# Half-width matmuls in an output projection, a strided operand in another, and some low parts on GpSimd, in a hybrid SSD and convolution decoder layer

## The chip, the cores and the metric

The kernel runs on one core of one Trainium2 chip. The metric is the device time of one execution in microseconds (us). Lower is better. Smaller durations are given in nanoseconds (ns).

## The reference, cut to what matters

One decoder layer is applied to 256 prompt tokens and 8 × 8 sample tokens, which the kernel treats as one set of 320 columns.

```python
x = x + 0.5 * rmsnorm(swiglu_ffn(rmsnorm(x, n_f1_pre), f1g, f1u, f1d), n_f1_post)
m = token_mixer(rmsnorm(x, n_mix_pre), ...)          # and new states
x = x + rmsnorm(m, n_mix_post)
x = x + 0.5 * rmsnorm(swiglu_ffn(rmsnorm(x, n_f2_pre), f2g, f2u, f2d), n_f2_post)

# the end of token_mixer
ssd_out = y @ w_ssd_out                               # y: the SSD scan's output, gated and normed
u = silu(layernorm(u, cc_ln_g, cc_ln_b))              # u: the convolution branch, 1024 channels
cc_out = u @ w_cc_out                                 # (320, 1024) @ (1024, 2048)
g_ssd, g_cc = split(sigmoid(gate_logits), 2)
out = (g_ssd * ssd_out + g_cc * cc_out) @ w_o         # (320, 2048) @ (2048, 2048)
```

The model width is 2048, the width of the feed-forward layers is 5632, and everything is float32.

## The kernel before, in words

**Layout.** Activations lie transposed: 128 channels on the partitions and the `T = 320` tokens along the free dimension. A matmul therefore has a 128 × 128 tile of weights as its stationary operand and 320 columns of activations as its moving operand, and writes 128 × 320 sums to one PSUM bank.

**Precision.** The product of two float32 matrices is made from float32r parts, which the tensor engine streams in one pass. Each operand is split into a high part (a copy rounded to float32r) and a low part (the difference). Three matmuls then make one product: high weights times high activations, low weights times high activations, high weights times low activations. In the code these are `hs` with `xh`, `ls` with `xh`, and `hs` with `xl`.

**Weights.** They are streamed once. SyncE issues a transfer of 512 KB into a buffer `raw` (three of them, each of two chunks of 512 columns). For each chunk ScalarE makes the high part `wh` (six buffers, `split_hi`) and VectorE the low part `wl` (five buffers, `split_lo`), which also ends the use of that half of `raw`. A chunk holds four weight tiles and so feeds 12 matmuls. `ensure` writes these instructions into the program several chunks ahead: when the matmuls of chunk c are written, high parts up to chunk c+6 and low parts up to c+4 have been written (line 210 and 212 issue the transfers).

**Phases.** `phase` runs a matrix product: a list of groups of output tiles (`groups`, mostly two at a time), an inner loop over the `nk` tiles of the contraction, and the three matmuls for each. A function `rhs(k)` names the moving operands and a function `evac` queues the work that empties the PSUM banks, of which there are four (`acc`). The order of phases is: feed-forward 1 in two halves (`w_up1a`, `w_dn1a`, `w_up1b`, `w_dn1b`), the input projections of the mixer, the SSD output projection (`WSSD`), the convolution's output projection (`OUT_16`, 8 tiles of contraction, operands `uh` and `ul` from `rhs_u`, emptied by `evac_cc`, which multiplies by the gate and adds the other branch), the final output projection (`WO`, 16 tiles of contraction, operands `ch` and `cl`, emptied by `evac_o` on ScalarE), and feed-forward 2 (`w_up2a`, `w_dn2a`, `w_up2b`, `w_dn2b`). After the last phase a tail normalizes and adds the result; six of its 16 additions run on GpSimd (line 1454).

**Order.** The order of instructions is written out by the program, with an own model of engine time that decides only where background work (the SSD scan and the convolutions) is placed. All instructions recorded through the wrapped engines carry line 78 in the profile, so tiles rather than lines tell them apart.

Of the kernel before, what the change touches and what calls it, by code (L numbers as in the profile page):

```python
# [6 lines left out]
F32 = mybir.dt.float32  # L7
F32R = mybir.dt.float32r
AF = mybir.ActivationFunctionType
ALU = mybir.AluOpType  # L10

D = 2048
KT = D // 128
T = 320
# [37 lines left out]
WO = [2] * 7 + [1, 1]  # L52


class Bank:
    def __init__(self, ap, now):
        self.ap, self.now = ap, now
        self._free = False
# [111 lines left out]
class Builder:  # L170
    def __init__(self, tc, io):
        self.tc, self.io = tc, io
        self.nc = Core(tc.nc)
        self.clock = self.nc.clock
        self.chunks = []
        for name in (
            "w_up1a", "w_dn1a", "w_up1b", "w_dn1b", "w_in1", "w_dt", "w_in2", "w_ssd", "w_cc", "w_o",
            "w_up2a", "w_dn2a", "w_up2b", "w_dn2b",
        ):
            if name == "w_dt":  # L180
                self.jdt = len(self.chunks)
            for i in range(io[name].shape[0]):
                w = io[name].shape[2]
                for c in range(0, w, CW):
                    self.chunks.append((io[name][i], c, w))
        self.nd = self.nh = self.nl = self.cc = 0
        self.raws, self.spl = {}, {}
        self.tasks, self.bg = [], []
        self.ready = set()
        self.due = []  # L190
        self.slack = 1.4
        self.tick = 0
# [32 lines left out]
    def split_lo(self, j):  # L225
        if j == self.jdt:
            h = self.spl[j][0]
            self.nc.vector.tensor_tensor(h[:, :, 32:64], self.raws.pop(j).rearrange("p (k c) -> p k c", c=32),
                                         h[:, :, 0:32].bitcast(F32), op=ALU.subtract)
            return  # L230
        l = self.wl.tile([128, CW], F32R, name="wl", tag="wl")
        self.nc.vector.tensor_tensor(l, self.raws.pop(j), self.spl[j][0].bitcast(F32), op=ALU.subtract)
        self.spl[j][1] = l

    def prefetch(self, upto):
# [82 lines left out]
        self.cur = self.spl.pop(c)  # L318
        self.cc += 1

    def phase(self, groups, nk, rhs, evac, on_k=None, width=128, on_last=None, mid=None):
        nc = self.nc
        u = 0
        m0 = 0
        per = CW // width
        for gi, G in enumerate(groups):
            if G <= 2:
                accs = [self.ring("acc") for _ in range(G)]
            else:
                accs = [self.ring(t) for t in ("acc", "acc", "acc", "acc", "m", "m", "m")[:G]]  # L330
            for k in range(nk):
                if gi == 0 and on_k is not None:
                    on_k(k)
                for j in range(G):
                    if gi == 0 and j == G - 3 and k == nk - 1 and mid is not None:
                        mid()
                    uu = u % per
                    if uu == 0:
                        self.boundary()
                    if u % 2 == 0:  # L340
                        self.tick += 1
                        self.step_bg()
                    h, l = self.cur
                    hs = h[:, uu * width : (uu + 1) * width]
                    ls = l[:, uu * width : (uu + 1) * width]
                    xh, xl = rhs(k)
                    a = accs[j].ap[:width, :T]
                    nc.tensor.matmul(a, lhsT=hs, rhs=xh, start=(k == 0), stop=False)
                    nc.tensor.matmul(a, lhsT=ls, rhs=xh, start=False, stop=False)
                    nc.tensor.matmul(a, lhsT=hs, rhs=xl, start=False, stop=(k == nk - 1))  # L350
                    u += 1
                if on_last is not None and gi == len(groups) - 1:
                    on_last(k)
            evac(gi, m0, accs)
            m0 += G
# [225 lines left out]
    def mixer(self, on_k):  # L581
        nc, io = self.nc, self.io
# [8 lines left out]
        G1 = lambda m: self.x[:, m]  # L591
# [698 lines left out]
        def rhs_u(k):  # L1290
            assert ("u", k) in self.ready
            uh, ul = st["u"]
            return uh[:, k], ul[:, k]

        ch = [unit("ch0", "A", F32R), unit("ch1", "B", F32R)]
        cl = [unit("cl0", "C", F32R), unit("cl1", "D", F32R)]
# [1 line left out]
        def evac_cc(gi, m0, accs):  # L1298
            def g(m, a):
                t = self.temp()  # L1300
                nc.vector.tensor_tensor(t, a.ap[:, :T], G1(m), op=ALU.mult)
                a.free = True
                nc.vector.tensor_tensor(t, t, G2(m), op=ALU.add)
                yield
                h, l = ch[m // 8][:, m % 8], cl[m // 8][:, m % 8]
                nc.scalar.activation(h, t, AF.Copy)
                yield
                nc.vector.tensor_tensor(l, t, h.bitcast(F32), op=ALU.subtract)
                self.ready.add(("comb", m))
            for i, a in enumerate(accs):  # L1310
                self.tasks.append(g(m0 + i, a))

        self.phase(OUT_16, 8, rhs_u, evac_cc)
        ym = [unit("ym0", "G"), unit("ym1", "H")]
        Y = lambda m: ym[m // 8][:, m % 8]
# [33 lines left out]
                        out=self.x[:, 4 * q : 4 * q + 4], in_=self.xd[:, 4 * q : 4 * q + 4]))  # L1349
            return rhs_c(k)  # L1350

        self.phase(WO, KT, rhs_c2, evac_o)
        self.preload(AF.Sqrt)
        self.flush()
        rb = self.rstd([self.acc_y, self.sq_last], 1.0 / D, keep=True)
# [238 lines left out]
```

## Time and profile before

| | |
|---|---|
| median of the timed runs | 2881.01 us (2 runs, 2880.92 and 2881.09) |
| profiled execution, span from first to last instruction | 2878.3 us |
| profiled execution's time around that span | not recorded; the timed runs' median lies 2.7 us above the span |
| TensorE matmuls | 19597, busy 2857.3 us |
| weight loads | 19597 |
| VectorE, ScalarE, GpSimd busy | 1709.1, 1336.2, 41.1 us |
| stage of `OUT_16` (first to last start) | 1751.7 to 1807.9 us |
| stage of `WO` | 1808.0 to 1920.5 us |
| low parts of `w_up2b` and `w_dn2b` | 2388.9 to 2851.8 us |

The engines of the profile are PE (TensorE's matmuls), PEld (its weight loads), DVE (VectorE), ACT (ScalarE), POOL (GpSimd) and SP (SyncE). A matmul's row shows its time from start to a modelled end, and matmuls overlap in the pipeline, so the pace is read from the distance between starts and not from the durations. A row such as `acc<-ch,wl 128*128 128x320` names the output, the operands, the size of the stationary operand and the size of the output.

### The profile page before, as it was taken

To read this page: it belongs to the slowest core of one execution; us is meant where nothing else is said; L and a number is where in the kernel's file an instruction comes from. 1 tells how busy PE (TensorE), PEld (TensorE's weight loads), DVE (VectorE), ACT (ScalarE), POOL (GpSimd) and SP (SyncE) were. 2 spreads that over 40 slices of the span, in tenths; PEclk is the share of its full clock that TensorE was granted. 3 is DMA by queue.
4 is the path that set the end of the run, shared out by engine and by line. 5 is a ranking of instruction groups with operands and counts; after the bars stand their busy time and mean duration, and the time that the engine had idled before them with its cause. 6 is when DMAs were issued, how large, how long until landed. Compare 5 with 4: busy or idle time off the path is not lost.

```text
span 2878.3 us, 50646 instructions
## 1 busy us (share of the span) xinstructions
PE 2857.3 (99%) x19597; PEld 2828.1 (98%) x19597; DVE 1709.1 (59%) x3374; ACT 1336.2 (46%) x2498; POOL 41.1 (1%) x81
## 2 busy tenths in 40 slices
PE   9999999999999999999999999999999999999998
PEld 9999999999999999999999999999999999999998
DVE  6555433555544887588989987557555434555444
ACT  6444333444444566456554544445444433444443
POOL 0000000000000000000000000000000000000000
PEclk9999999999999999999999999999999999999999
DMA  6444444444444545665566645544444444444443
GB/s 203 149 150 151 149 152 148 153 148 152 149 150 151 173 149 188 214 221 190 179 197 224 203 147 169 169 132 147 149 152 147 153 147 151 150 149 152 148 153 118
DMA packets 132705, 465.84 MB, mean 162 GB/s; under 512 B 15360, under 2 KB 17200, under 8 KB 132464
## 3 DMA queue, kind: packets, MB, share of 16 engines
q1 hardware_dynamic: 126880, 441.94, 48.7%
q0 software_dynamic: 5584, 20.67, 2.1%
q8 instruction: 153, 2.51, 0.4%
q14 instruction: 88, 0.72, 0.1%
HBM read 443.77 MB, written 18.78 MB: 161 GB/s over the span
## 4 chain that ended last, share of the span: by engine, by line
PE 99%; DVE 1%; ACT 0%; DMA 0%; issue 0%; SPq 0%
PE acc L78 93%; PE m L78 5%; PE n L78 1%; DVE t L78 0%; DMA x<-x 0%; DVE x L78 0%; DVE st L78 0%; ACT xgh L78 0%; ACT L78 0%; ACT t L78 0%; ACT wh L78 0%; SPq L210 0%; DVE wl L78 0%; ACT st L78 0%; DVE yy L78 0%
## 5 line engine op out<-in xcount | busy, mean ns | idle before, releaser
L78 DVE TENSOR_TENSOR wl<-raw,wh 128x512 fp32r<-128x512 f32 x1568 | 1080.0, 690 | 1108.3 <-PE acc L78 974.9
L78 ACT ACTIVATE wh<-raw 128x512 fp32r<-128x512 f32 x1568 | 987.6, 632 | 1466.7 <-PE acc L78 1391.7
L78 PE MATMUL acc<-xgh,wh 128*128 128x320 f32 x4240 | 1318.3, 311 | 8.9 <-ACT wh L78 5.5
L78 PE MATMUL acc<-xgl,wh 128*128 128x320 f32 x4240 | 1312.5, 310 | 0.0
L78 PE MATMUL acc<-xgh,wl 128*128 128x320 f32 x4240 | 1312.4, 310 | 0.1
L78 PEld LDWEIGHTS acc<-xgh,wh 128*128 128x128 f32 x4240 | 798.3, 188 | 14.7 <-ACT wh L78 6.3
L78 PEld LDWEIGHTS acc<-xgh,wl 128*128 128x128 f32 x4240 | 798.3, 188 | 2.9 <-issue 1.0
L78 PEld LDWEIGHTS acc<-xgl,wh 128*128 128x128 f32 x4240 | 798.0, 188 | 0.9 <-DVE xgl L78 0.9
L78 PE MATMUL acc<-hl,wh 128*128 128x320 f32 x1408 | 435.2, 309 | 0.0
L78 PE MATMUL acc<-hh,wl 128*128 128x320 f32 x1408 | 435.2, 309 | 0.0
L78 PE MATMUL acc<-hh,wh 128*128 128x320 f32 x1408 | 435.2, 309 | 0.0
L78 PEld LDWEIGHTS acc<-hh,wh 128*128 128x128 f32 x1408 | 264.3, 188 | 0.0
L78 PEld LDWEIGHTS acc<-hh,wl 128*128 128x128 f32 x1408 | 264.3, 188 | 0.0
L78 PEld LDWEIGHTS acc<-hl,wh 128*128 128x128 f32 x1408 | 264.3, 188 | 0.0
L78 DVE SCALAR_TENSOR_TENSOR cvo<-pad,cw,cvo 128x256 f32<-128x256 f32 x480 | 152.2, 375 | 0.0
L78 DVE TENSOR_TENSOR t<-acc,rb 128x320 f32<-128x320 f32 x212 | 93.8, 482 | 2.1 <-ACT rb L78 2.1
L78 PE MATMUL acc<-ch,wl 128*128 128x320 f32 x256 | 79.1, 309 | 0.0
L78 PE MATMUL acc<-ch,wh 128*128 128x320 f32 x256 | 79.1, 309 | 0.0
L78 PE MATMUL acc<-cl,wh 128*128 128x320 f32 x256 | 79.1, 309 | 0.0
L78 PE MATMUL m<-xgh,wh 128*128 128x320 f32 x240 | 75.4, 314 | 0.0
L78 PE MATMUL m<-xgh,wl 128*128 128x320 f32 x240 | 75.0, 313 | 0.1
L78 PE MATMUL m<-xgl,wh 128*128 128x320 f32 x240 | 74.8, 312 | 0.0
(206 smaller groups left out, 1566.6 us busy)
## 6 DMA issues: line engine op xcount, KB each, us to landing
raw<-w_in SPq DMA_DIRECT2D x176, 512.0 KB, 3.6
raw<-w_up1b SPq DMA_DIRECT2D x88, 512.0 KB, 3.5
raw<-w_up2a SPq DMA_DIRECT2D x88, 512.0 KB, 3.5
raw<-w_up2b SPq DMA_DIRECT2D x88, 512.0 KB, 3.5
raw<-w_up1a SPq DMA_DIRECT2D x85, 512.0 KB, 3.6
raw<-w_dn1a SPq DMA_DIRECT2D x44, 512.0 KB, 3.5
raw<-w_dn1b SPq DMA_DIRECT2D x44, 512.0 KB, 3.5
raw<-w_dn2a SPq DMA_DIRECT2D x44, 512.0 KB, 3.5
```

The costliest lines, as they stand in the source:

```text
L78: return f(*a, **k)
```

## The change

There are three edits.

1. The final output projection (`WO`) calls `phase` with `halves=True`. Each of its three matmuls for a weight tile becomes two, over columns 0 to 159 and 160 to 319, with the same weights one after the other.
2. In the convolution's output projection (`OUT_16`) the moving operand is read as all even columns and then all odd columns, with a step of two float32 elements (8 bytes). The sums come out in that order, and `evac_cc` reads them back from PSUM in the order of tokens.
3. For the chunks of `w_up2b` and `w_dn2b`, every fourth low part (`j % 4 == 0`) is made by GpSimd and not by VectorE. `jpool` is the number of the first chunk of `w_up2b`.

```diff
+            if name == "w_up2b":
+                self.jpool = len(self.chunks)
...
         l = self.wl.tile([128, CW], F32R, name="wl", tag="wl")
-        self.nc.vector.tensor_tensor(l, self.raws.pop(j), self.spl[j][0].bitcast(F32), op=ALU.subtract)
+        eng = self.nc.gpsimd if j >= self.jpool and j % 4 == 0 else self.nc.vector
+        eng.tensor_tensor(l, self.raws.pop(j), self.spl[j][0].bitcast(F32), op=ALU.subtract)
...
-                    nc.tensor.matmul(a, lhsT=hs, rhs=xh, start=(k == 0), stop=False)
-                    nc.tensor.matmul(a, lhsT=ls, rhs=xh, start=False, stop=False)
-                    nc.tensor.matmul(a, lhsT=hs, rhs=xl, start=False, stop=(k == nk - 1))
+                    if halves:
+                        for i, (w, x) in enumerate(((hs, xh), (ls, xh), (hs, xl))):
+                            for t0 in (0, T // 2):
+                                nc.tensor.matmul(a[:, t0 : t0 + T // 2], lhsT=w, rhs=x[:, t0 : t0 + T // 2],
+                                                 start=(k == 0 and i == 0 and t0 == 0),
+                                                 stop=(k == nk - 1 and i == 2 and t0 > 0))
+                    else:
...
         def rhs_u(k):
             assert ("u", k) in self.ready
             uh, ul = st["u"]
-            return uh[:, k], ul[:, k]
+            odd = lambda ap: ap.rearrange("p (a b) -> p b a", b=2)
+            return odd(uh[:, k]), odd(ul[:, k])
...
-                nc.vector.tensor_tensor(t, a.ap[:, :T], G1(m), op=ALU.mult)
+                pair = lambda ap: ap.rearrange("p (a b) -> p a b", b=2)
+                nc.vector.tensor_tensor(pair(t), a.ap[:, :T].rearrange("p (b a) -> p a b", b=2), pair(G1(m)), op=ALU.mult)
...
-        self.phase(WO, KT, rhs_c2, evac_o)
+        self.phase(WO, KT, rhs_c2, evac_o, halves=True)
```

More of the change, by code (lines that the diff above doesn't have):

```diff
@@ L319, in boundary, with phase @@
         self.cc += 1
-    def phase(self, groups, nk, rhs, evac, on_k=None, width=128, on_last=None, mid=None):
+    def phase(self, groups, nk, rhs, evac, on_k=None, width=128, on_last=None, mid=None, halves=False):
         nc = self.nc
@@ L347, in phase @@
                     a = accs[j].ap[:width, :T]
-                    nc.tensor.matmul(a, lhsT=hs, rhs=xh, start=(k == 0), stop=False)
-                    nc.tensor.matmul(a, lhsT=ls, rhs=xh, start=False, stop=False)
-                    nc.tensor.matmul(a, lhsT=hs, rhs=xl, start=False, stop=(k == nk - 1))
+                    if halves:
[5 more added lines that the diff above has]
+                    else:
+                        nc.tensor.matmul(a, lhsT=hs, rhs=xh, start=(k == 0), stop=False)
+                        nc.tensor.matmul(a, lhsT=ls, rhs=xh, start=False, stop=False)
+                        nc.tensor.matmul(a, lhsT=hs, rhs=xl, start=False, stop=(k == nk - 1))
                     u += 1
```

## The prediction

> **What bounds the kernel now.** The first view is the page: span, busy time by engine, and the chain of work that ended last.
>
> ```profile
> span 2878.3 us, 50646 instructions
> ...
> PE 2857.3 (99%) x19597; PEld 2828.1 (98%) x19597; DVE 1709.1 (59%) x3374; ACT 1336.2 (46%) x2498; POOL 41.1 (1%) x81
> ...
> PE 99%; DVE 1%; ACT 0%; DMA 0%; issue 0%; SPq 0%
> ```
>
> The chain is TensorE for 99% of the span. Matmuls and weight loads have the same count, so each matmul brings a load of its own. Busy time does not say which of the two sets the pace, so I read starts. The two stages that the change touches on TensorE come next: the instructions of one tile with their first and last start, and the busy time in each stretch.
>
> ```profile
> L78 PEld LDWEIGHTS acc<-ch,wh x256: 187/188/188, 1807.9 to 1920.1; 128*128 128x128 f32 x128
> L78 PE MATMUL acc<-ch,wh x256: 308/309/310, 1808.0 to 1920.2; 128*128 128x320 f32 x128
> L78 PE MATMUL acc<-ul,wh x128: 309/309/314, 1752.0 to 1807.9; 128*128 128x320 f32 x128
> ...
> 1808.03:1921.00 112.97, 112.97 (x774) 112.97 (x772) 52.96 (x84) 52.79 (x97) 0.53 (x1) 1.00 0.50 156
> 1751.71:1808.03 56.32, 56.32 (x386) 56.32 (x385) 41.33 (x78) 25.28 (x46) 1.60 (x3) 1.00 0.58 185
> ```
>
> In the final projection 255 rounds of three matmuls take 1920.2 − 1808.0 = 112.2 us, so one matmul starts every 0.1467 us and the stage is 768 × 0.1467 = 112.6 us. The convolution's projection gives (1807.9 − 1752.0) / 127 / 3 = 0.1467 us too, and 384 of them make 56.3 us. The columns after the matmuls are loads, VectorE (53 of 113 us, and 41 of 56), ScalarE and GpSimd; the granted clock is 1.00. TensorE alone sets both stages.
>
> What does a matmul's 0.1467 us consist of? Two views: the mixer's `wdt` tile, with narrow weights, and the timeline around one matmul of 512 columns.
>
> ```profile
> L78 PEld LDWEIGHTS acc<-xgh,wdt x16: 133/134/136, 1006.1 to 1010.6; 128*64 128x64 f32 x16
> L78 PE MATMUL acc<-xgh,wdt x16: 303/306/311, 1006.3 to 1010.8; 128*64 128x320 f32 x16
> L78 PEld LDWEIGHTS acc<-xgl,wdt x16: 107/108/109, 1006.3 to 1010.5; 128*32 128x32 f32 x16
> ...
> 1250.04 0.40 PE L78 MATMUL m<-hu 96*128 96x512 f32 x1
> 1250.28 0.32 PE L78 MATMUL acc<-xgh,wh 128*128 128x320 f32 x1
> ```
>
> With 64 and 32 weight columns instead of 128, a pair still takes (1010.8 − 1006.3) / 15 = 0.30 us, 0.15 each: at 320 columns the load is hidden. The 512-column matmul holds the next one off for 0.24 us; 0.1467 × 512 / 320 is 0.235. So the time is proportional to the columns streamed, about 0.458 ns each, with no fixed part visible. 160 columns would stream in 0.0733 us.
>
> The load, then, must be sized. The timeline of weight loads shows them where nothing streams long enough to cover them:
>
> ```profile
> 55.60 0.53 PEld L78 LDWEIGHTS n<-ones,acc_sq 128*128 128x128 f32 x4
> ...
> 56.05 0.19 PEld L78 LDWEIGHTS acc<-xgh,wh 128*128 128x128 f32 x1
> 56.16 0.19 PEld L78 LDWEIGHTS acc<-xgh,wl 128*128 128x128 f32 x1
> 56.31 0.19 PEld L78 LDWEIGHTS acc<-xgl,wh 128*128 128x128 f32 x1
> ...
> 58.48 0.19 PEld L78 LDWEIGHTS m<-xgh,wh 128*128 128x128 f32 x1
> 58.59 0.19 PEld L78 LDWEIGHTS m<-xgh,wl 128*128 128x128 f32 x1
> ```
>
> The first row is four loads ahead of matmuls of one column: (0.53 − 0.19) / 3 = 0.113 us apart. Those weights are plain float32. But the kernel's own float32r weights show the same where a stream begins: the second load starts 0.11 us after the first (56.16 and 56.05, 58.59 and 58.48), and only the third waits for a matmul (56.31, 0.15 later). A third way: 134 − 108 = 26 ns for 32 more columns and 188 − 134 = 54 ns for 64 more is 0.84 ns a column, 108 ns for 128.
>
> **The change part by part.**
>
> *Half-width matmuls.* Removed: 768 matmuls and loads. Added: 1536 of each, every matmul with 160 columns. Loads run beside the matmul before them, so the pace is the larger of stream and load: the larger of 0.073 and 0.112. I take 0.112 (between 0.11 and 0.113, the rows with 128-column loads back to back). 1536 × 0.112 = 172.0 us, minus 112.6: **+59.4 us**, all on the path. Ends: 0.108 gives 165.9, +53.3; 0.114 gives 175.1, +62.5. Below nothing: the columns streamed stay the same, so the stage has no gain to make. What is queued behind: VectorE and ScalarE are half idle here, the parts of weights are released by TensorE, and they only come later with it.
>
> [...]
>
> *Strided moving operand.* 384 matmuls of unchanged width. No row shows a moving operand with a step. Lower end: nothing, as the same 320 columns stream and the output is written in one run. Upper end: if what is fetched comes in runs of neighbours and half of each is now thrown away, the stream doubles: 384 × 0.1467 = **+56.3 us**. The float32r stream is already slower than a plain-float32 pass would suggest:
>
> ```profile
> 2860.47 1.24 PE L78 MATMUL m<-x,cw 128*128 128x320 f32 x4
> ...
> L78 PE MATMUL acc<-x,cw 128*128 128x320 f32 x6 | 1.9, 433 | 0.0
> ```
>
> Four plain-float32 passes over 320 columns start (1.24 − 0.43) / 3 = 0.27 us apart, 0.84 ns a column; half of that would be 0.42, and float32r takes 0.458. That tenth could be a limit of the operand's read, which speaks for the upper end. I take nothing, since the nearest row is the same stream of 320 columns without a step and a tenth is far from a doubling, and leave 0.35 to the upper end.
>
> [...]
>
> The evacuation reads PSUM in runs of two. Nearest rows:
>
> ```profile
> L78 DVE TENSOR_TENSOR t<-acc,x 128x320 f32<-128x320 f32 x16 | 7.7, 483 | 0.0
> L78 DVE TENSOR_TENSOR dp<-acc,rb 128x256 f32<-128x256 f32 x17 | 7.0, 414 | 0.0
> L78 DVE TENSOR_TENSOR dp<-acc,rb 128x64 f32<-128x64 f32 x17 | 3.6, 212 | 0.0
> ```
>
> The last, in runs of eight, costs (414 − 212) / 192 = 1.05 ns a column like the plain one, so runs cost nothing there. If 483 ns doubled, 16 × 0.483 = 7.7 us would be added to VectorE's 41 of 56 us, which still fits: nothing.
>
> *Low parts on GpSimd.* 264 chunks (the row below), every fourth: 66 move.
>
> ```profile
> L78 DVE TENSOR_TENSOR wl<-raw,wh x264: 679/692/695, 2388.9 to 2851.8; 128x512 fp32r<-128x512 f32 x132
> ...
>   PE acc L78: 208.3, 210
> ...
> L1454 POOL TENSOR_TENSOR x<-x,t 128x320 f32<-128x320 f32 x6 | 5.0, 861 | 1055.9 <-DVE t L78 1055.0 <-ACT x L78 0.9
> ...
> 2869.66 2.50 POOL L1454 TENSOR_TENSOR x<-x,t 128x320 f32<-128x320 f32 x3 [0.88 <-ACT x L78]
> ...
> 2871.55 0.96 DVE L78 TENSOR_TENSOR x<-x,t 128x320 f32<-128x320 f32 x1
> 2872.95 0.49 DVE L78 TENSOR_TENSOR x<-x,t 128x320 f32<-128x320 f32 x1
> ```
>
> GpSimd takes 861 ns for 320 columns, at most 1.6 × 861 = 1.38 us for 512. It also holds VectorE up: in the tail an addition took 0.96 us beside GpSimd's (2869.66 to 2872.16) and 0.49 right after. So count 1.38 us for GpSimd's parts, and up to 0.69 + 1.38 = 2.07 for a VectorE one beside it. The cover: a low part waits for a TensorE buffer (210 of 264 times). With five buffers the one just freed is needed four chunks later, 4 × 12 × 0.1467 = 7.0 us. 2.07 fits. Its cost is nothing; without that cover each would cost 0.7 us, 66 × 0.7 = 46 us.
>
> The move also ends the use of `raw` later, and SyncE's next transfer waits for that:
>
> ```profile
> SPq L212 <- DVE wl L78: 347.9, 112, 3.5
> ...
> raw<-w_up2b SPq DMA_DIRECT2D x88, 512.0 KB, 3.5
> ...
> 2500.51 0.33 SPq L212 DMA_DIRECT2D raw<-w_up2b  x1
> ...
> 2506.95 0.63 ACT L78 ACTIVATE wh<-raw 128x512 fp32r<-128x512 f32 x1 [1.12 <-PE acc L78]
> ```
>
> The transfer issued at 2500.51 fills the tile whose first high part ScalarE makes at 2506.95 (the fifth high part after that low part, by the order of `ensure`). 6.44 − 3.5 = 2.9 us to spare; 0.7 to 2.1 later still lands in time. Nothing else queues on GpSimd in this stage. The 66 × 0.692 = 45.7 us that VectorE saves lie beside TensorE and gain nothing.
>
> **Sum.** Span 2878.3 + 59.4 = 2937.7. The profile gives the execution no time beyond its span; the timed median 2881.0 is 2.7 above it, and I keep that: **2940 us**, 2.0% slower. About 2% is what a measurement of this kernel can tell from no change, 57.6 us here, so the sum sits on that line.
>
> **The rivals.**
>
> *Both edits cost* (load bound, and doubled stream): 2881.0 + 59.4 + 56.3 = 2997. For it: the tenth above. Against: no row shows doubling.
>
> *The load stays hidden*, the side that is not slower: the array keeps the tile for the second half, or a load needs less than 0.073 us, the point from which it decides. Then the stage stays at 1536 × 0.0733 = 112.6 us and the time at 2881; a load between 0.073 and 0.108 us would put it between that and 2934. Against it: 19597 loads for 19597 matmuls, and 0.11 us in three places. With a doubled stream it gives 2937. [...]
>
> *Narrow float32r matmuls fall to the pace of plain float32*: two passes of 0.27 us for 320 columns are 0.27 us for 160; 1536 × 0.27 = 414.7, +302: 3183. For it: no float32r matmul here has fewer than 320 columns. Against it: nothing in the rows makes width matter.
>
> **How the numbers follow.** Load bound 0.78, hidden 0.12, float32 pace 0.10; step free 0.65, doubled 0.35. Forecast 0.78 × 0.65 = 0.51 at 2934 to 2944; both edits 0.27 at 2991 to 3000; hidden and free 0.08 at 2881 or somewhat above; hidden with a doubled stream 0.04 at 2937; float32 pace 0.10 at 3183 or above. The range 2929 to 3000 holds the first two and the fourth, 0.82; the forecast's own is 2930 to 2946. Slower by over 2% (above 2938.6): 0.6 of the forecast, 0.31, with 0.27, 0.10 and 0.02, so 0.70. Within 2%: 0.29. Faster: 0.01.
>
> **What the profile after would show.** Rows of `ch` with x512 and 128x160, 0.112 us apart, over 172 us, with loads back to back; 0.073 apart would prove the load hidden, 0.27 the float32 pace. Rows of `uh` 0.147 apart if the step is free, 0.293 if not. GpSimd rows of `wl` x66 of 1.4 us or less, VectorE rows of `wl` in the same stretch partly longer, and no gap before `hh,wl` or `xgh,wl` matmuls; gaps there would make the third part wrong. A granted clock under 1.00 in the last projection would add to its time and prove the pace wrong for another reason.

## The result and the profile after

The changed kernel takes 2990.98 us (2990.90 to 2991.06) against 2881.01, a ratio of 1.0381 with a 95% interval of 1.0364 to 1.0398. It is slower by 110 us. The profiled execution took 2990.9 us, with a span of 2989.1, so 1.8 us lie around the span.

The page of the changed kernel, span and busy time by engine:

```profile
span 2989.1 us, 52279 instructions
...
PE 2968.2 (99%) x20365; PEld 2910.9 (97%) x20365; DVE 1670.2 (56%) x3308; ACT 1337.2 (45%) x2498; POOL 126.5 (4%) x147
...
PE 99%; DVE 0%; ACT 0%; DMA 0%; issue 0%; POOLq 0%
```

There are 768 more matmuls and 768 more loads: no load was left out for a second half with the same weights. TensorE still makes 99% of the chain, so the 110 us are time of matmuls. The busy time in stretches says which. First the kernel before, then the changed one, each cut at the start of the convolution's projection, the start of the final projection and its end (columns: stretch, length, then busy time and count of PE, PEld, DVE, ACT and POOL, granted clock, DMA share and rate):

```profile
0.00:1751.71 1751.71, 1742.38 (x12038) 1717.85 (x12039) 1131.88 (x2384) 855.53 (x1647) 33.88 (x71) 1.00 0.53 170
...
1808.03:1920.70 112.67, 112.67 (x771) 112.67 (x770) 52.96 (x84) 52.49 (x97) 0.53 (x1) 1.00 0.50 156
1920.70:2878.30 957.60, 945.96 (x6409) 941.28 (x6408) 482.93 (x828) 402.93 (x709) 5.05 (x6) 0.99 0.47 146
```

```profile
0.00:1752.06 1752.06, 1742.31 (x12037) 1718.53 (x12038) 1132.55 (x2384) 855.71 (x1647) 33.88 (x71) 1.00 0.50 170
1752.06:1860.84 108.78, 108.78 (x387) 79.98 (x385) 42.08 (x79) 25.21 (x46) 1.61 (x3) 1.00 0.32 101
1860.84:2032.40 171.56, 171.56 (x1538) 171.56 (x1537) 53.05 (x84) 53.81 (x98) 0.53 (x1) 1.00 0.30 102
2032.40:2989.10 956.70, 945.51 (x6409) 940.83 (x6408) 442.54 (x762) 402.49 (x707) 90.54 (x72) 0.99 0.44 146
```

The stage of the convolution's projection grew from 56.3 to 108.8 us (+52.5) and that of the final projection from 112.7 to 171.6 (+58.9). Ahead of them 0.4 us was added, and behind them 0.9 us less was spent. Together that is 110.8, the difference of the spans. The two small ones are no larger than the differences between executions of one kernel, and nothing ties them to an edit. VectorE's busy time in the two stages hardly changed (41.3 to 42.1, and 53.0 to 53.1 us) and the granted clock stayed at 1.00.

The tiles of the two stages in the changed kernel, with duration and first and last start:

```profile
L78 PEld LDWEIGHTS acc<-ch,wh x512: 192/192/209, 1860.6 to 2031.7; 128*128 128x128 f32 x171
L78 PE MATMUL acc<-ch,wh x512: 259/275/278, 1860.8 to 2031.8; 128*128 128x160 f32 x171
...
L78 PEld LDWEIGHTS acc<-ul,wh x128: 207/208/209, 1752.3 to 1860.3; 128*128 128x128 f32 x128
L78 PE MATMUL acc<-ul,wh x128: 465/466/466, 1752.6 to 1860.6; 128*128 128x320 f32 x128
```

In the final projection 512 matmuls of this kind, a third of the stage, run from 1860.8 to 2031.8: 171.0 / 1531 = 0.1117 us from one start to the next. In the convolution's projection (1860.6 − 1752.6) / 127 / 3 = 0.283 us. Since the stage before the change had 0.1467, the stream of 320 columns went from 0.458 to 0.885 ns a column.

### The profile page after: what moved, and what is told of

It reads as the page before. It is cut to its first block, busy times and chain, and to the rows that moved or that the text cites. A ratio compares the mean times of both kernels' runs of the same rounds, so it can differ in the third digit from the quotient of the medians.

```text
span 2989.1 us, 52279 instructions
## 1 busy us (share of the span) xinstructions
PE 2968.2 (99%) x20365; PEld 2910.9 (97%) x20365; DVE 1670.2 (56%) x3308; ACT 1337.2 (45%) x2498; POOL 126.5 (4%) x147
## 4 chain that ended last, share of the span: by engine, by line
PE 99%; DVE 0%; ACT 0%; DMA 0%; issue 0%; POOLq 0%
PE acc L78 93%; PE m L78 5%; PE n L78 1%; DVE t L78 0%; DMA cw<-cw 0%; DVE x L78 0%; DVE st L78 0%; ACT xgh L78 0%; ACT t L78 0%; DVE wl L78 0%; ACT st L78 0%; ACT wh L78 0%; ACT ym L78 0%; DVE yy L78 0%; POOLq L1584 0%
## 5 line engine op out<-in xcount | busy, mean ns | idle before, releaser
L78 DVE TENSOR_TENSOR wl<-raw,wh 128x512 fp32r<-128x512 f32 x1502 | 1035.4, 691 | 1253.9 <-PE acc L78 1128.4
L235 POOL TENSOR_TENSOR wl<-raw,wh 128x512 fp32r<-128x512 f32 x66 | 85.5, 1295 | 1014.8 <-PE acc L78 986.0
L78 PE MATMUL acc<-ch,wh 128*128 128x160 f32 x512 | 99.6, 275 | 0.0
L78 PE MATMUL acc<-cl,wh 128*128 128x160 f32 x512 | 99.5, 275 | 0.0
L78 PE MATMUL acc<-ch,wl 128*128 128x160 f32 x512 | 99.4, 275 | 0.0
L78 PEld LDWEIGHTS acc<-ch,wh 128*128 128x128 f32 x512 | 77.9, 192 | 0.1
L78 PEld LDWEIGHTS acc<-ch,wl 128*128 128x128 f32 x512 | 77.8, 192 | 0.0
```

The costliest lines, as they stand in the source:

```text
L78: return f(*a, **k)
L235: eng.tensor_tensor(l, self.raws.pop(j), self.spl[j][0].bitcast(F32), op=ALU.subtract)
```

## The experiments

All kernels start from the one before the change, and a row of a table gives the median and the ratio to the kernel before that ran beside it. In the diffs, only what differs is shown.

### Each edit alone

`e1_halves` has the first edit alone (`halves` in `phase`), `e2_step2` the second (in `rhs_u` and `evac_cc`), `e3_gpsimd` the third (`jpool` and the line in `split_lo`), each as printed above.

```diff
# e1_halves
-        self.phase(WO, KT, rhs_c2, evac_o)
+        self.phase(WO, KT, rhs_c2, evac_o, halves=True)
# e2_step2
-            return uh[:, k], ul[:, k]
+            odd = lambda ap: ap.rearrange("p (a b) -> p b a", b=2)
+            return odd(uh[:, k]), odd(ul[:, k])
# e3_gpsimd
+        eng = self.nc.gpsimd if j >= self.jpool and j % 4 == 0 else self.nc.vector
```

> The first edit alone: the final output projection in 160-column matmuls. Theory (the load sets the pace): a matmul every 0.1117 us as in the changed kernel, the stage takes 171.5 us instead of 112.6, the time is 2881.0 + 58.9 = 2939.9 us. Rival (part of the loss in the changed kernel came from what the strided stage before left behind, or from the two edits together): the stage takes less than 171.5 us alone, and the time lies well under 2935 us.

> The second edit alone: the convolution's projection with a moving operand of step 2. Theory (the operand's read sets the pace): 0.2833 us for each of 384 matmuls, the stage takes 108.8 us instead of 56.3, the time is 2881.0 + 52.5 = 2933.5 us. Rival (it is the evacuation, which reads PSUM in runs of two, that holds the stage up): TensorE would show idle time or waits for VectorE in the stage, and the rows of the evacuation would be longer than 483 ns.

> The third edit alone: every fourth low part of the last two weight matrices on GpSimd. Theory (7.0 us of cover for 1.29 us of work): 2881 us, within 1 us. Rival (the parts on GpSimd arrive late, or hold VectorE up): each of the 66 costs up to 0.6 us, 2881 to 2921 us, with gaps on TensorE after 2389 us.

| kernel | us | ratio, 95% interval |
|---|---|---|
| `e1_halves` | 2940.08 | 1.0204 (1.0188 to 1.0219) |
| `e2_step2` | 2933.08 | 1.0180 (1.0163 to 1.0197) |
| `e3_gpsimd` | 2881.24 | 0.9999 (0.9990 to 1.0008) |

The kernel before stood at 2881.16 beside them, so the edits cost 58.9, 51.9 and 0.1 us, 110.9 in all against the 110.0 of the changed kernel: the parts add up to the whole within 1 us, and each does alone what it does with the others. The rows of the tiles, `e1_halves` first and `e2_step2` second, show the same pace as in the changed kernel: (1979.7 − 1808.7) / 1531 = 0.1117 us and (1859.7 − 1751.8) / 127 / 3 = 0.283.

```profile
L78 PE MATMUL acc<-ch,wh x512: 237/275/278, 1808.7 to 1979.7; 128*128 128x160 f32 x171
```

```profile
L78 PE MATMUL acc<-uh,wh x128: 442/465/466, 1751.8 to 1859.7; 128*128 128x320 f32 x128
```

The evacuation now takes its elements in turn from the first and the second half of the 320 sums, 160 columns (640 bytes) apart in PSUM. It takes as long as the plain one did before (483 ns), so the rival for the second edit falls (groups by shape, `e2_step2`):

```profile
L78 DVE TENSOR_TENSOR t<-acc,x 128x320 f32<-128x320 f32 x16 | 7.7, 483 | 0.0
```

### Is it the load or the width of the matmul?

```diff
# e4_w64; e7_w96 has 96 in place of 64
+                            n = 128 if (k, i) in ((0, 0), (nk - 1, 2)) else 64
...
+                                nc.tensor.matmul(a[:n, t0 : t0 + T // 2], lhsT=w[:, :n], rhs=x[:, t0 : t0 + T // 2],
```

> The first edit with 64 instead of 128 weight columns in all but the first and last of the three-matmul steps, which leaves out half of the final projection's sums. The streams stay at 160 columns, 1536 of them; only the load is halved. Theory (the load sets the pace): a load of 64 columns takes about 0.84 x 64 = 54 ns and hides behind a stream of 0.0733 us, so 1472 matmuls at 0.0733 and 64 at 0.112 make 115 us, and the time is about 2883.5 us. Rival (a matmul of under some number of columns has a pace of its own, whatever the load): still 0.112 us each, 2940 us.

> The first edit with 96 instead of 128 weight columns in all but the first and last of the three-matmul steps, which leaves out a quarter of the final projection's sums. Theory (pace is the larger of the stream, 0.075 us, and a load proportional to its columns): 0.1117 x 96 / 128 = 0.084 us, 1472 of them and 64 at 0.112 make 131 us, 2881 + 18 = 2899 us. Rival (a load under 128 columns is hidden or has a fixed time): 0.075 us and 2886 us as with 64 columns, or 0.112 us and 2940 us.

`e4_w64` took 2885.80 us (ratio 1.0016, 1.0006 to 1.0026) and `e7_w96` 2900.33 (1.0067, 1.0046 to 1.0089). The tile's rows, `e4_w64` first:

```profile
L78 PEld LDWEIGHTS acc<-ch,wl x512: 133/135/140, 1808.8 to 1926.3; 128*64 128x64 f32 x171
L78 PE MATMUL acc<-ch,wl x512: 233/237/245, 1808.9 to 1926.3; 128*64 128x160 f32 x171
```

```profile
L78 PEld LDWEIGHTS acc<-ch,wl x512: 164/165/165, 1810.0 to 1941.7; 128*96 128x96 f32 x171
L78 PE MATMUL acc<-ch,wl x512: 244/247/251, 1810.1 to 1941.8; 128*96 128x160 f32 x171
```

With 64 weight columns the 1536 matmuls of 160 columns take 117.9 us, 0.0768 each on average with the 64 wide ones among them, so (117.9 − 64 × 0.112) / 1472 = 0.0752 for the narrow ones. That is the stream, with 2 ns on top of 160 × 0.458 that I had not counted; over 1472 matmuls that is 2.8 us, and the measured time lies 2.3 us above the 2883.5 expected. With 96 columns it is (132.2 − 7.2) / 1472 = 0.0849 us, where 0.1117 × 96 / 128 gives 0.0838. The same 160 columns thus take 0.075, 0.085 and 0.112 us with 64, 96 and 128 columns of weights. With 96 and 128 columns of weights the pace is that of the load, and the 160 columns as such have no slower pace of their own. Fewer weight columns also mean fewer rows of sums written to PSUM, and these two runs change both together. But in the kernel before, 128 rows of 320 sums took 0.1467 us a matmul, so half as many sums are no reason for 0.112, while loads alone come 0.11 us apart where no matmul holds them up, as the prediction's timeline shows.

### What in the strided operand costs?

The first four of these change only the order in which the convolution's projection streams its 320 columns, and `evac_cc` reads them back to match (its lines are left out here). The last two take the operand two columns further on, or two back for the last tile of the contraction, so that it stays within the tensor; this changes the sums and not the amount of work. In `e12_runs4_off` `evac_cc` is that of `e10_runs4`, in `e11_off` it is the plain one.

```diff
# e5_step4: one column, three skipped, in four passes
+            odd = lambda ap: ap.rearrange("p (a b) -> p b a", b=4)
# e6_pairs: runs of c = 2 and gaps of 2, in two passes; e10_runs4 has c=4, e9_runs80 c=80
+            odd = lambda ap: ap.rearrange("p (a b c) -> p b a c", b=2, c=2)
# e12_runs4_off: runs of 4, all of it 8 bytes further on
+            o = k * T + (2 if k < 7 else -2)
+            odd = lambda q: q.rearrange("p k t -> p (k t)")[:, o : o + T].rearrange("p (a b c) -> p b a c", b=2, c=4)
# e11_off: one run, 8 bytes further on
+            off = lambda q: q.rearrange("p k t -> p (k t)")[:, o : o + T]
```

> The second edit alone with a step of four elements (16 bytes) instead of two: the 320 columns in four passes of 80. Theory A (operands are fetched 8 bytes at a time, and a step of 8 bytes already wastes half of each fetch): no worse than a step of two, 0.283 us a matmul, 2933 us. Theory B (they are fetched in lines of 16 bytes, at a fixed time for each line, of which a step of two uses half): one column in each line, 0.57 to 0.59 us a matmul, 384 x 0.44 = 169 us more than before, 3040 to 3050 us. Theory C (any moving operand that isn't one run is slow): 0.283 us, 2933 us.

> The second edit alone with pairs of neighbours: two columns (8 bytes), then a gap of 8 bytes, in two passes. Theory A (fetches of 8 bytes): each fetch is used in full, 0.147 us a matmul, 2881 us. Theory B (lines of 16 bytes at a fixed time): half of each line is used, 0.283 us, 2933 us. Theory C (any moving operand that isn't one run is slow): 0.283 us or more, 2933 us or more.

> The second edit with runs of 80 neighbours in the order first, third, second, fourth: as many dimensions in the operand's pattern as the pairs had, but only three breaks in 320 columns. Theory C1 (any moving operand that isn't one run streams at 0.283 us): 2933 us. Theory C2 (what costs is breaks between neighbours, or short runs): 0.147 to 0.150 us, 2881 to 2882 us.

> The second edit with runs of four neighbours (16 bytes) and gaps of 16 bytes, in two passes. Theory B' (reads in lines of 16 bytes, each line used in full here): 0.147 us a matmul, 2881 us. Theory C1 (any operand that isn't one run): 0.283 us, 2933 us. Theory C2 (a cost for each break): half the breaks of the pairs, 160 x (0.283 - 0.147) / 160 halved, 0.215 us a matmul, 2907 us.

> Runs of four neighbours as in the run before, but the whole operand taken two columns (8 bytes) further along its tile, so that each run of 16 bytes lies half in one line of 16 bytes and half in the next. The convolution's projection then works on columns shifted by two, which changes its values and not its amount of work. Theory L (fetches are aligned lines of 16 bytes and the quick stream needs all four of a line): 0.283 us a matmul, 2933 us. Theory R (the quick stream needs runs of four, wherever they start): 0.147 us, 2881 us.

> The operand in one run as before the change, but starting two columns (8 bytes) further along its tile; values shifted in the same way. Theory L and theory R alike: all but the first and last line are used in full, 0.147 us a matmul, 2881 us. Rival (an operand has to start on a line): 0.283 us, 2933 us.

| kernel | columns in a run | of each 16 bytes, taken in one pass | us a matmul | us | ratio, 95% interval |
|---|---|---|---|---|---|
| before | 320 | all | 0.147 | 2881 | |
| `e9_runs80` | 80 | all | 0.147 | 2880.75 | 0.9999 (0.9987 to 1.0010) |
| `e10_runs4` | 4 | all | 0.147 | 2880.88 | 0.9999 (0.9988 to 1.0011) |
| `e11_off` | 320, from 8 bytes on | all | 0.147 | 2880.91 | 1.0000 (0.9989 to 1.0011) |
| `e6_pairs` | 2 | half, two neighbours | 0.283 | 2933.22 | 1.0181 (1.0160 to 1.0203) |
| `e2_step2` | 1, step 2 | half | 0.283 | 2933.08 | 1.0180 (1.0163 to 1.0197) |
| `e12_runs4_off` | 4, from 8 bytes on | half, twice | 0.286 | 2934.64 | 1.0186 (1.0156 to 1.0215) |
| `e5_step4` | 1, step 4 | a quarter | 0.290 | 2935.98 | 1.0191 (1.0169 to 1.0213) |

The pace is read from these rows, of `e9_runs80`, `e10_runs4`, `e11_off`, `e12_runs4_off`, `e6_pairs` and `e5_step4` in that order, as the distance from the first to the last start over 127 × 3 = 381. For `e10_runs4` it is (1808.3 − 1752.4) / 381 = 0.147, for `e12_runs4_off` (1862.2 − 1753.1) / 381 = 0.286, for `e6_pairs` (1859.6 − 1751.6) / 381 = 0.283 and for `e5_step4` (1861.9 − 1751.5) / 381 = 0.290.

```profile
L78 PE MATMUL acc<-uh,wh x128: 307/308/308, 1751.9 to 1807.7; 128*128 128x320 f32 x128
```

```profile
L78 PE MATMUL acc<-uh,wh x128: 307/308/308, 1752.4 to 1808.3; 128*128 128x320 f32 x128
```

```profile
L78 PE MATMUL acc<-uh,wh x128: 305/311/312, 1752.7 to 1808.6; 128*128 128x320 f32 x128
```

```profile
L78 PE MATMUL acc<-uh,wh x128: 443/465/468, 1753.1 to 1862.2; 128*128 128x320 f32 x128
```

```profile
L78 PE MATMUL acc<-uh,wh x128: 443/466/467, 1751.6 to 1859.6; 128*128 128x320 f32 x128
```

```profile
L78 PE MATMUL acc<-uh,wh x128: 451/474/475, 1751.5 to 1861.9; 128*128 128x320 f32 x128
```

Each run threw out a theory. The pairs of neighbours cost as much as single columns, so fetches of 8 bytes (theory A) fall. The four runs of 80, in a pattern of as many dimensions as the pairs had, are free, and so are the runs of four: an operand in several runs is not slow as such (theory C, and C1), and the number of breaks has no price (C2, which gave 0.215 for runs of four). The runs of four that start 8 bytes later are slow again (0.286), with the same evacuation, while one long run with the same offset is free (0.147). So what decides in these runs is whether the stream takes all four columns of each line of 16 bytes as it comes to it (0.147 us a matmul) or not (0.283 to 0.290). Lines are counted here from the start of the operand's tile; where that lies in memory no row shows. Theory B had the line but not the price: a quarter of a line (0.290) costs hardly more than half (0.283), where a fixed time for each line would have made it 0.57 or more. Below a full line the stream falls to about 0.9 ns a column, with half or a quarter of the line nearly alike (0.885 and 0.906). Why it is one lower pace, and why it is this one, stays open. It lies near the 0.84 ns a column of the plain-float32 passes in the prediction, but no run tests whether the two have one cause.

### How far does GpSimd's cover reach?

```diff
# e8_gpsimd_all
+        eng = self.nc.gpsimd if j >= self.jpool else self.nc.vector
```

> The third edit taken to its end: all 264 low parts of the last two weight matrices on GpSimd, none on VectorE. Theory (the cover is real: 1.29 us of work for each chunk, which TensorE uses up in 12 x 0.1467 = 1.76 us, and 7.0 us ahead): 2881 us, within 2 us, with GpSimd busy for 342 of 463 us. Rival (GpSimd and VectorE hold each other up, so that parts or emptied banks come late): each chunk 0.2 to 0.5 us later than it is used, 53 to 130 us more, 2935 to 3010 us.

2881.07 us, ratio 1.0000 (0.9990 to 1.0009): the cover holds all 264. The rows of GpSimd and of two VectorE operations, from the tile's rows and the groups by shape of `e8_gpsimd_all`:

```profile
L235 POOL TENSOR_TENSOR wl<-raw,wh x264: 1283/1295/1503, 2390.2 to 2853.1; 128x512 fp32r<-128x512 f32 x132
```

```profile
L78 DVE TENSOR_TENSOR t<-acc,rb 128x320 f32<-128x320 f32 x41 | 19.0, 491 | 175.6 <-PE acc L78 175.6
L78 DVE TENSOR_TENSOR acc_sq<-acc_sq,t 128x320 f32<-128x320 f32 x14 | 14.6, 1043 | 20.2 <-ACT t L78 20.2
```

VectorE is held up behind 2389 us, but only where both operands lie in SBUF: `acc_sq` takes 1043 ns on average instead of 486 (all 102 of the kernel before), while `t<-acc,rb`, which reads one operand from PSUM, stays at 491. GpSimd's parts (a median of 1295 ns, the longest 1503) end well inside the 1.76 us that TensorE needs for a chunk. In the kernel before TensorE is busy for all of the stretch from 2389 to 2853 us (464.0 of 464.0), and the time with 264 parts is the same.

## Why the prediction was right or wrong

The range held the time, but the forecast did not: 2991 against 2940. What happened is the first rival, both edits costing, which stood at 2997 with a chance of 0.27; the range held because it had been drawn wide enough for that rival, and not because the mechanism forecast was right.

- **The load sets the pace of the half-width matmul.** Right in mechanism and size: 0.1117 us against 0.112, +58.9 against +59.4. `e4_w64` and `e7_w96`, together with the 0.11 us between uncovered loads, show that it is the load. The two rivals to this step fell: the load is not hidden and not left out for a second half (20365 loads for 20365 matmuls, 0.112 apart), and there is no pace of plain float32 for a narrow matmul (0.075 us in `e4_w64`).
- **A step of two in the moving operand costs nothing.** This is the step that failed. I took nothing, because the nearest row was the same stream without a step, and left 0.35 to the doubling. It measured +52.5 us in the stage, just under the upper end of 56.3 (0.283 us a matmul instead of 0.293). That the upper end came so near is partly luck. In its mechanism the time grows with the share of each fetch that is thrown away: with fetches of 8 bytes the pairs would have been free, and with fetches of 16 bytes one column of four would have taken 4 × 0.1467 = 0.587 us. `e6_pairs` took 0.283 and `e5_step4` 0.290. What the runs show in its place is one lower pace as soon as a line of 16 bytes is not taken whole: two of its four columns cost 0.283 us a matmul and one 0.290, all four 0.147, and the same runs of four begun 8 bytes later 0.286 (`e6_pairs`, `e5_step4`, `e10_runs4`, `e12_runs4_off`). The sign that I had quoted, a float32r stream a tenth slower than half a plain pass, pointed the same way, but no run shows that this tenth comes from the operand's read, and that half a plain pass is the measure for a float32r stream was my guess.
- **The evacuation costs nothing.** Right: 483 ns before and after. It was misread, though: it has no runs of two in PSUM, but takes single elements 640 bytes apart in turn, so the row with runs of eight was not as near a case as the prediction makes it.
- **Low parts on GpSimd cost nothing.** Right: 2881.24 us alone. 1294 ns each, inside the 1.38 us of the bound, and even four times as many are covered. One thing came out otherwise: I expected VectorE's own low parts to be longer beside GpSimd's. In the changed kernel they are not (693 ns against 692): most of them wait for a buffer that TensorE frees, one comes free every 1.76 us, and GpSimd's part is done in 1.29 (at most 1.34). The ones held up are other operations with two operands in SBUF, and few of them: `hl` and `acc_sq` rise to means of 535 and 702 ns, from 486 and 488 (groups by shape of the changed kernel behind 2500 us):

```profile
L78 DVE TENSOR_TENSOR wl<-raw,wh 128x512 fp32r<-128x512 f32 x198 | 137.1, 693 | 270.8 <-PE acc L78 250.6 <-PE m L78 11.9 <-issue 3.4
...
L78 DVE TENSOR_TENSOR hl<-t,hh 128x320 fp32r<-128x320 f32 x22 | 11.6, 535 | 0.4 <-ACT hh L78 0.4
...
L78 DVE TENSOR_TENSOR acc_sq<-acc_sq,t 128x320 f32<-128x320 f32 x14 | 9.8, 702 | 2.7 <-ACT t L78 2.3
```

- **Transfers that wait for GpSimd's parts land in time.** Right: SyncE waited for them (second row), and ScalarE's high parts wait for TensorE as before and for no transfer.

```profile
ACT wh L78 <- PE acc L78: 252.9, 241, 1.4
...
SPq L214 <- POOL wl L235: 157.8, 64, 2.8
```

- **The sum.** The 2.7 us kept around the span came from two different executions, a timed median and the span of a profiled one. Wherever the record has time and span of the same execution, of the kernel before or of any other, 1.8 to 2.1 us lie around the span; in the changed kernel's profiled one it was 1.8. So some 0.6 to 0.9 us of the 2.7 is a difference between executions, and that is about what separates the 110.8 us of the spans from the 110.0 of the times.

## What to carry to other kernels

Where every matmul brings its own weights, read the distance between two loads in the timeline at a place where no stream covers them: a matmul that streams for less than that is paid as a load, and cutting it in two pays the load twice (160 columns here: 0.075 us of stream, 0.112 of load). Reorder or stride a float32r moving operand only in whole lines of 16 bytes, four columns at a time, as in the runs that cost nothing here (0.147 us a matmul; with parts of lines 0.283 to 0.290). Work moved to a slower engine was free here because its duration (1.29 us) stayed under the period in which its result is used up (1.76 us), and because the engine that it holds up had time to spare (VectorE is busy for 442.5 us of the 956.7 behind the final projection).

## What had not been expected of the hardware

A moving operand that takes only part of each 16-byte line streams at one lower pace, 0.885 ns a column with half of a line and 0.906 with a quarter, against 0.458 with all of it. Runs of 16 bytes cost nothing where they start on a line, counted from the start of the tile (0.147 us a matmul); 8 bytes off they cost 0.286. GpSimd's parts took as long with 264 of them as with 66 (medians of 1295 and 1294 ns, the longest 1503 and 1336). It was some of VectorE's operations with two SBUF operands that took longer, by up to 1.1 us (`hl<-t,hh` at most 1591 ns in the changed kernel, 487 before), and those with one operand in PSUM hardly did (`t<-acc,rb` a mean of 491 ns in `e8_gpsimd_all`, 481 before).
